# A one-layer encoder block on one core: the experts of the last 32 tokens by gathered rows, and a weight-stationary expert output stage for the other 224

## The chip, the core and the metric

The kernel runs on one core of a Trainium2 chip. The metric is device time in microseconds. The kernel is written in a tile framework: the Python code allocates tiles from pools of buffers and issues operations, and a scheduler gives each engine its fixed order of instructions. Engines: TensorE (PE; its weight loads are listed as PEld), VectorE (DVE), ScalarE (ACT), GpSimd (POOL) and SyncE (SP), which issues the loads of the weights.

## What is computed

One layer on 256 tokens of 2048 features: two token mixers, cross-attention to 256 memory tokens, and a feed-forward layer of 16384 experts of one neuron each, of which every token takes 8 x 16 = 128. The last of these matters here:

```python
def peer_ffn(a, w_pq, sub_keys, expert_u, expert_v):
    ...
    expert = (i1 * PEER_KEYS + i2).astype(jnp.int32)      # T x 8 x 16
    gate = jax.nn.softmax(best_s, axis=-1).astype(t.dtype)
    ...
        u = expert_u[eb]
        pre = jnp.einsum('bd,bed->be', xb, u)
        act = jax.nn.gelu(pre.astype(jnp.float32), approximate=False).astype(xb.dtype) * gb
        return jnp.einsum('be,bed->bd', act, expert_v[eb])
```

`expert_u` and `expert_v` have 16384 rows of 2048 float32 each (134 MB each). The result is added to `h`, and a last RMSNorm follows.

## The kernel before

Every product with weights goes through `wtile` (L82): a tile of 128x2048 float32 (1 MB) is loaded by SyncE's queue into `w` (three buffers), ScalarE casts it to `wh` (L92), and the residual `wl` = `w` - `wh` is formed by VectorE (L94); for the expert input tiles 0 to 63 VectorE takes 1536 columns and GpSimd the other 512 (L97). `wh` and `wl` have two buffers each. The other operand is split in the same way into a high and a low part, and three of the four partial products are summed in PSUM. A number behind `wl` is that of its tile in the order of the code: `wl185` is U's first before and after, and V begins with `wl250` before and `wl252` after.

The experts are computed densely, for all 16384 and all 256 tokens. The input stage U (`u_steps`, L740) runs over 128 tiles of 128 experts. For each of 16 slices of features a pair of matmuls has the weights loaded and the tokens streamed: `wh` against the high and low part of the normed tokens `aT` side by side (512 columns), and `wl` against the high part (256 columns). GELU gives a tile of `P`, 128 experts x 256 tokens; 16 of these make `P0` to `P7`. Beside tiles 0 to 31 the selection of the experts runs on VectorE (`select_steps`), beside tiles 32 to 63 the gates are laid out as a dense matrix (`gate_steps`): one-hot vectors of both halves of an expert's number, eight tokens at a time, f16 matmuls of 128 columns, and stores to the DRAM tensor `gd`. `run_spread` hands out the side work evenly.

The output stage V (`v_steps`, L825) runs over 16 groups `c` of 1024 experts and four slices of 512 features, two weight tiles for each. `gate(c)` (L810) loads the gates of a group and multiplies `P` by them, and the product is split into `ah` and `al`. Here the tokens are the loaded operand and the weights are streamed: 24 matmuls of 512 columns a tile, and VectorE adds the result to `h` after every second tile. The order is U tiles 0 to 63, V quarter 0 (32 tiles), U 64 to 95, V quarter 1, U 96 to 127, V quarters 2 and 3, and the final norm.

Of the kernel before, what the change touches and what calls it, by code (L numbers as in the profile page):

```python
# [9 lines left out]
F32 = mybir.dt.float32  # L10
# [17 lines left out]
TB = 8  # L28


@with_exitstack
def block_kernel(ctx: ExitStack, tc: tile.TileContext, a: dict, out: bass.AP):
# [4 lines left out]
    big = ctx.enter_context(tc.tile_pool(name="big", bufs=6))  # L37
    mid = ctx.enter_context(tc.tile_pool(name="mid", bufs=6))
# [22 lines left out]
    h = const.tile([P, 2, D], F32, tag="h", name="h")  # L61
# [109 lines left out]
    def transpose_split(src, k0, nk, dst, name, gi=None):  # L171

        for kp in range(nk // 2):
# [11 lines left out]
            for kk in range(2):  # L185
                g = gcols[:, gi, k + kk : k + kk + 1]
                ps = pt[:, kk * S : (kk + 1) * S]
                last = nc.scalar.activation(dst[0][:, k + kk, :], ps, AF.Copy, scale=g).ins
                nc.vector.scalar_tensor_tensor(
                    dst[1][:, k + kk, :], ps, g, dst[0][:, k + kk, :].bitcast(F32), op0=ALU.mult, op1=ALU.subtract  # L190
                )
        return last if gi is not None else None

    class Both:


        def __init__(self, name):
            self.tiles = [X([P, NK // 2, 2, S], F32R, f"{name}{i}") for i in range(2)]
# [17 lines left out]
    def norm_steps(name, src, r, gi, dst):  # L216

        xn = X([P, 2, D], F32, f"xn_{name}")
        for q in range(4):
# [3 lines left out]
            transpose_split(xn[:, :, f], 4 * q, 4, dst, name, gi)  # L223
# [225 lines left out]
    def residual(name, w, xT_, ssq_, sides):  # L449

        for f in range(4):
            fs = slice(f * 512, (f + 1) * 512)

            def done(b, ps):
                nc.vector.tensor_tensor(h[:, b, fs], h[:, b, fs], ps, op=ALU.add)
                sumsq(h, b, f, ssq_)

# [152 lines left out]
    residual("mo", a["mem_w_o"], oT, ssq, sides)  # L610
# [8 lines left out]
    gT = const.tile([P, 2, S], F16, tag="gT", name="gT")  # L619
# [30 lines left out]
    aT = Both("a")  # L650
    side = raw_steps("hf", 3, gT_, 3)
    norm = norm_steps("ffn", h, rf_, 3, aT)
# [20 lines left out]
    def select_steps(b):  # L673
# [37 lines left out]
        for s in range(2):  # L711
            for hq in range(4):
# [11 lines left out]
                yield  # L724
        pt = pst(f"pt_sel{b}")
# [3 lines left out]
        t = slice(b * P, (b + 1) * P)  # L729
        nc.vector.tensor_copy(i1T[:, t], pt[:, 0:P])  # L730
        nc.vector.tensor_copy(i2T[:, t], pt[:, P : 2 * P])

        nc.vector.tensor_scalar(gT[:, 0, t], pt[:, 2 * P : 3 * P], GSCALE, None, op0=ALU.mult)
        nc.vector.scalar_tensor_tensor(
            gT[:, 1, t], pt[:, 2 * P : 3 * P], GSCALE, gT[:, 0, t], op0=ALU.mult, op1=ALU.subtract
        )
        yield

# [3 lines left out]
    def u_steps(q):  # L742

        for j in range(32 * q, 32 * q + 32):
            if j % 16 == 0:
                ptiles[j // 16] = X([P, 16, S], F32, f"P{j // 16}")
# [8 lines left out]
            nc.scalar.copy(pre, po[:, S : 2 * S])  # L755
            nc.vector.tensor_tensor(pre, po[:, 0:S], pre, op=ALU.add)  # L756
            nc.scalar.activation(pre, pre, AF.Gelu)  # L757
            yield


    gd = dram.tile([P, 16, 16, 8, 16], F32, tag="gd", name="gd")

    def gate_steps():


        def onehots(t0):
# [5 lines left out]
            o1 = small.tile(sh, F16, tag="o1", name=f"o1_{t0}", bufs=2)  # L772
            eq = small.tile(sh, F16, tag="eq", name=f"eq_{t0}", bufs=1)
# [10 lines left out]
        for t0 in range(0, S, TB):  # L784
# [3 lines left out]
            for q in range(2):  # L788
                ps = psm(f"ps_g{t0}_{q}")
                for n in range(4):  # L790
                    t = 4 * q + n
                    for i in range(2):
                        nc.tensor.matmul(  # L793
                            ps[:, n * P : (n + 1) * P], o1[:, t // 2, :, t % 2], o2[:, i, t // 2, :, t % 2], start=(i == 0), stop=(i == 1)
# [12 lines left out]
            if t0 + TB < S:  # L807
# [3 lines left out]
    def gate(c):  # L811

        n_w[0] += 1
        g = stream.tile([P, 16, 8, 16], F32, tag="w", name=f"w{n_w[0]}", bufs=3)
        nc.sync.dma_start(g, gd[:, c])
        for e in range(2):
            for j in range(4):
                pv = ptiles[c // 2][:, c % 2 * 8 + 4 * e + j, :].rearrange("p (b t) -> p b t", b=16)
                nc.vector.tensor_tensor(pv, pv, g[:, :, 4 * e + j, :], op=ALU.mult)

    ssq_f = new_ssq("final")
    gf = None

    def v_steps(q):

        nonlocal gf
        for c in range(4 * q, 4 * q + 4):
            if c == 15:
                gf = X([P, D], F32, "gf")
                bcast_rows(gf, a["g_final"])  # L830
            ah, al = [], []
            for e in range(2):
                j = 8 * c + 4 * e
                src = ptiles[j // 16][:, j % 16 : j % 16 + 4, :]
                ah.append(M([P, 4, S], F32R, f"ah{c}_{e}"))
                al.append(M([P, 4, S], F32R, f"al{c}_{e}"))
                split(ah[e], al[e], src)
            for ds in range(4):
                po = [acc(f"v{c}_{ds}_{b}") for b in range(2)]
                for e in range(2):  # L840
                    wh, wl = wtile(a["peer_vP"][(c * 4 + ds) * 2 + e], 0)
                    wh = wh.rearrange("p (j f) -> p j f", j=4)
                    wl = wl.rearrange("p (j f) -> p j f", j=4)
                    for j in range(4):
                        for b in range(2):
                            t = slice(b * P, (b + 1) * P)
# [97 lines left out]
```

## Time and profile before

| | us |
|---|---|
| median of 3 runs | 2573.64 |
| lowest, highest | 2573.09, 2575.64 |
| the profiled execution | 2572.24 |
| its span in the trace | 2570.5 |
| TensorE busy | 2540.2 |
| VectorE, ScalarE, GpSimd busy | 1568.8, 1166.1, 176.8 |

The span is cut by its stages: the selection beside U tiles 0 to 31 starts at 1096 us, the gate matrix beside U tiles 32 to 63 fills 1297 to 1481, the first V quarter 1500 to 1674, the third quarter of U 1674 to 1855, and the last V tile ends at about 2558 us. In the rows further down, "PE" is the matmul stream and "PEld" the weight loads, which overlap it. Matmuls are pipelined, so the distance between the starts of two neighbours tells the pace, not the length of one. "idle before" of an engine is time between two of its instructions, with the instruction that released it.

### The profile page before, as it was taken

How to read it: one execution, taken by the hardware profiler on the slowest of the kernel's cores; microseconds unless marked ns; L12 is line 12 of the kernel's file. 1: busy time of each engine (PE TensorE's matmuls, PEld its weight loads, DVE VectorE, ACT ScalarE, POOL GpSimd, SP SyncE). 2: the span in 40 equal slices, each digit the busy share in tenths (PEclk: the TensorE clock that was granted, in tenths of full speed). 3: DMA queues.
4: the chain of work that ended last, by engine and by line, in shares of the span. 5: the costliest groups of instructions: out<-in, count | busy, mean ns of one | idle time of the engine just before them, and what ended most of it. 6: DMA issues, size and time to landing. Idle time of an engine off the chain costs nothing. (4 is left out here: it accounts for less than half of the span.)

```text
span 2570.5 us, 32130 instructions
## 1 busy us (share of the span) xinstructions
PE 2540.2 (99%) x13266; PEld 2158.1 (84%) x13266; DVE 1568.8 (61%) x1877; ACT 1166.1 (45%) x1310; POOL 176.8 (7%) x124
## 2 busy tenths in 40 slices
PE   8999999999999999999999999999999999999998
PEld 7888888888888888888888888888888888888886
DVE  5556544456555455899679866544566544666665
ACT  5454434545444345454455544344443344434443
POOL 0000000000000000022444410000000000000000
PEclk9999999999999999999999999999999999999999
DMA  6554555554544545445567765555565555655663
GB/s 248 186 201 169 182 193 194 215 193 168 191 170 166 177 174 179 168 170 180 181 223 243 245 239 213 207 186 183 211 223 207 193 184 193 233 210 212 229 225 135
DMA packets 74050, 507.66 MB, mean 197 GB/s; under 512 B 8336, under 2 KB 8336, under 8 KB 15152
## 3 DMA queue, kind: packets, MB, share of 16 engines
q1 hardware_dynamic: 67904, 482.37, 52.5%
q0 software_dynamic: 5856, 23.20, 2.9%
q8 instruction: 104, 1.70, 0.3%
q14 instruction: 42, 0.34, 0.0%
q10 hardware_dynamic: 144, 0.03, 0.0%
HBM read 486.70 MB, written 18.87 MB: 197 GB/s over the span
## 5 line engine op out<-in xcount | busy, mean ns | idle before, releaser
L94 DVE TENSOR_TENSOR wl<-w,wh 128x2048 fp32r<-128x2048 f32 (+2 forms) x400 | 863.5, 2164 | 787.2 <-ACT wh L92 787.0
L92 ACT CAST wh<-w 128x2048 fp32r<-128x2048 f32 (+2 forms) x464 | 842.8, 1821 | 911.0 <-PE v L849 362.5
L752 PE MATMUL u<-a,wh 128*128 128x512 f32 x2048 | 725.2, 399 | 0.0
L753 PE MATMUL u<-a,wl 128*128 128x256 f32 x2048 | 574.5, 281 | 5.5 <-DVE wl L97 5.5
L752 PEld LDWEIGHTS u<-a,wh 128*128 128x128 f32 x2048 | 384.6, 188 | 91.5
L850 PE MATMUL v<-wl,ah 128*128 128x512 f32 x1024 | 398.5, 389 | 0.0
L848 PE MATMUL v<-wh,ah 128*128 128x512 f32 x1024 | 398.4, 389 | 0.0
L849 PE MATMUL v<-wh,al 128*128 128x512 f32 x1024 | 398.4, 389 | 0.0
L753 PEld LDWEIGHTS u<-a,wl 128*128 128x128 f32 x2048 | 386.4, 189 | 8.0 <-DVE wl L97 7.9
L850 PEld LDWEIGHTS v<-wl,ah 128*128 128x128 f32 x1024 | 192.2, 188 | 40.3 <-DVE wl L94 0.3
L849 PEld LDWEIGHTS v<-wh,al 128*128 128x128 f32 x1024 | 192.2, 188 | 39.9
L848 PEld LDWEIGHTS v<-wh,ah 128*128 128x128 f32 x1024 | 192.2, 188 | 39.9
L757 ACT ACTIVATE P<-P 128x256 f32<-128x256 f32 x128 | 53.5, 418 | 271.4 <-DVE P L756 271.4
L97 POOL TENSOR_TENSOR wl<-w,wh 128x512 fp32r<-128x512 f32 x64 | 134.8, 2105 | 318.1 <-ACT wh L92 307.1
L97 DVE TENSOR_TENSOR wl<-w,wh 128x1536 fp32r<-128x1536 f32 x64 | 112.6, 1760 | 50.2 <-ACT wh L92 50.2
L854 DVE TENSOR_TENSOR h<-h,v 128x512 f32<-128x512 f32 x128 | 85.2, 684 | 32.6 <-PE v L850 32.6
L116 PE MATMUL g<-wh,x 128*128 128x512 f32 x256 | 100.2, 391 | 0.0
L118 PE MATMUL g<-wl,x 128*128 128x512 f32 x256 | 99.6, 389 | 0.0
L117 PE MATMUL g<-wh,x 128*128 128x512 f32 x256 | 99.6, 389 | 0.0
L138 PE MATMUL qk<-x,wh 128*128 128x512 f32 x256 | 91.0, 400 | 0.2 <-DVE qk L144 0.2
L138 PE MATMUL pq<-hf,wh 128*128 128x512 f32 x256 | 91.0, 399 | 0.0
L138 PE MATMUL mq<-hq,wh 128*128 128x512 f32 x256 | 90.6, 398 | 0.0
(283 smaller groups left out, 3342.8 us busy)
## 6 DMA issues: line engine op xcount, KB each, us to landing
w<-in_peer_uT SPq DMA_DIRECT2D x128, 1024.0 KB, 4.8
w<-in_peer_vP SPq DMA_DIRECT2D x128, 1024.0 KB, 4.8
w<-in_w_in SPq DMA_DIRECT2D x72, 1024.0 KB, 4.8
w<-in_mem_w_kv SPq DMA_DIRECT2D x32, 1024.0 KB, 4.7
w<-in_w_out SPq DMA_DIRECT2D x16, 1024.0 KB, 4.7
w<-in_mem_w_q SPq DMA_DIRECT2D x16, 1024.0 KB, 4.7
w<-in_mem_w_o SPq DMA_DIRECT2D x16, 1024.0 KB, 4.8
w<-in_peer_w_q SPq DMA_DIRECT2D x16, 1024.0 KB, 4.7
```

The lines of the kernel that those rows point to most:

```text
L92: nc.scalar.copy(wh[:, c], w[:, c])
L94: nc.vector.tensor_tensor(wl[:, c], w[:, c], wh[:, c].bitcast(F32), op=ALU.subtract)
L97: e.tensor_tensor(wl[:, c], w[:, c], wh[:, c].bitcast(F32), op=ALU.subtract)
L116: nc.tensor.matmul(po[b], xh, wh[:, k, :], start=(kk == 0), stop=False)
L117: nc.tensor.matmul(po[b], xl, wh[:, k, :], start=False, stop=False)
L118: nc.tensor.matmul(po[b], xh, wl[:, k, :], start=False, stop=(kk == nkc * 4 - 1))
L138: nc.tensor.matmul(po[f], wh[:, k, fs], xT.both(kk), start=(kk == 0), stop=False)
L752: nc.tensor.matmul(po, wh[:, k, :], aT.both(k), start=(k == 0), stop=False)
L753: nc.tensor.matmul(po[:, 0:S], wl[:, k, :], aT[0][:, k, :], start=False, stop=(k == NK - 1))
L848: nc.tensor.matmul(po[b], ah[e][:, j, t], wh[:, j, :], start=first, stop=False)
L849: nc.tensor.matmul(po[b], al[e][:, j, t], wh[:, j, :], start=False, stop=False)
L850: nc.tensor.matmul(po[b], ah[e][:, j, t], wl[:, j, :], start=False, stop=last)
```

## The change

Tokens are divided: `SP` = 32 of them, the last, and `T` = 224.

The 224 stay dense. The matmuls of U have 448 and 224 columns, and `gate_steps` makes 28 groups of one-hot vectors and not 32. `v_steps` now loads the expert weights and streams the tokens: four PSUM tiles of 128 features x 224 tokens, 48 matmuls of 224 columns a weight tile, added by VectorE to `yT` (features x tokens) after every fourth tile. Behind the last tile `yT` is transposed and added to `hx`. `h` is stored to DRAM (`hd`) and reloaded as `hx` late in V; its buffers, and those of `P0` and `P1` (stored to `pd` and reloaded for V's last quarter), go to other tiles. V takes the groups in the order 2, 3, 4, 5, 6, 7, 0, 1 of `P`. `prep_steps` multiplies by the gates and splits for a whole `P` tile (16 tiles of experts) ahead of its use.

The 32 tokens are taken by rows. Partition 32g + t holds token t and a quarter g of its 128 experts, so that 32 steps cover them. Each step gathers 128 rows of `peer_u` by an indirect DMA from GpSimd's queue (1 MB), and VectorE multiplies them by the normed tokens with a sum along the row; after GELU and gate 32 more steps gather rows of `peer_v` and add them, scaled, to one accumulator, which a matmul with `fold` sums over the four quarters into `hx`. Three buffers hold gathered rows (`rows0`'s second half and both halves of `rows1`). `select_steps(1)` now runs ahead of `select_steps(0)` and writes the list of rows and gates `sx`. `run_spread` hands out the 65 steps over the first 168 tiles from V's first on.

```diff
-    big = ctx.enter_context(tc.tile_pool(name="big", bufs=6))
-    mid = ctx.enter_context(tc.tile_pool(name="mid", bufs=6))
+    big = ctx.enter_context(tc.tile_pool(name="big", bufs=7))
+    mid = ctx.enter_context(tc.tile_pool(name="mid", bufs=8))
...
+    def rows_of(src, k):
+        g = bufs[k % 3]
+        nc.gpsimd.indirect_dma_start(
+            g, None, src, bass.IndirectOffsetOnAxis(sx[:, 0, k : k + 1].bitcast(U32), 0)
+        )
+        return g
+
+    def sparse_input():
+        two = [X([P, 2, D], F32, f"rows{i}") for i in range(2)]
+        bufs.extend((two[0][:, 1], two[1][:, 0], two[1][:, 1]))
+        xs = two[0][:, 0]
...
+        nc.vector.scalar_tensor_tensor(xs, xs, rs, gb, op0=ALU.mult, op1=ALU.mult)
+        return xs
+
+    def sparse_steps(xs):
+        for k in range(SP):
+            g = rows_of(a["peer_u"], k)
+            nc.vector.tensor_tensor_reduce(
+                g, g, xs, 1.0, 0.0, op0=ALU.mult, op1=ALU.add, accum_out=act[:, k : k + 1]
+            )
...
+        y = xs
+        for k in range(SP):
+            g = rows_of(a["peer_v"], k)
+            ak = act[:, k : k + 1]
+            if k == 0:
+                nc.vector.tensor_scalar(y, g, ak, None, op0=ALU.mult)
+            else:
+                nc.vector.scalar_tensor_tensor(y, g, ak, y, op0=ALU.mult, op1=ALU.add)
+            yield
...
             for k in range(NK):
-                nc.tensor.matmul(po, wh[:, k, :], aT.both(k), start=(k == 0), stop=False)
-                nc.tensor.matmul(po[:, 0:S], wl[:, k, :], aT[0][:, k, :], start=False, stop=(k == NK - 1))
+                nc.tensor.matmul(po[:, 0 : 2 * T], wh[:, k, :], aT.both(k), start=(k == 0), stop=False)
+                nc.tensor.matmul(po[:, 0:T], wl[:, k, :], aT.tiles[k // 8][:, k % 8, 0], start=False, stop=(k == NK - 1))
...
+    def prep_steps(c):
...
+                nc.vector.tensor_tensor(pv, pv, g[:, :, j, :], op=ALU.mult)
+            yield
+        for e in range(4):
...
+            split(ah, al, pv)
+            parts[c, e] = (ah, al)
+            yield
...
-                    for j in range(4):
-                        for b in range(2):
-                            t = slice(b * P, (b + 1) * P)
-                            first, last = e == 0 and j == 0, e == 1 and j == 3
-                            nc.tensor.matmul(po[b], ah[e][:, j, t], wh[:, j, :], start=first, stop=False)
-                            nc.tensor.matmul(po[b], al[e][:, j, t], wh[:, j, :], start=False, stop=False)
-                            nc.tensor.matmul(po[b], ah[e][:, j, t], wl[:, j, :], start=False, stop=last)
...
+                    for f in range(4):
+                        fs = slice(f * P, (f + 1) * P)
+                        o = po[f][:, 0:T]
+                        for j in range(4):
+                            first, last = e == 0 and j == 0, e == 3 and j == 3
+                            nc.tensor.matmul(o, wh[:, j, fs], ah[:, j, :], start=first, stop=False)
+                            nc.tensor.matmul(o, wh[:, j, fs], al[:, j, :], start=False, stop=False)
+                            nc.tensor.matmul(o, wl[:, j, fs], ah[:, j, :], start=False, stop=last)
...
+    run_spread(u_steps(0), 31, chain(side, select_steps(1), select_steps(0)), 4 + 18 + 18)
+    xs = sparse_input()
+    run_spread(u_steps(1), 27, gate_steps(), T // TB + 1)
+    run(prep_steps(2))
+    rest = chain(
+        v_steps(0),
...
+    run_spread(rest, 168, sparse_steps(xs), 2 * SP + 1)
```

What the scheduler makes of it is another order than the code's. On VectorE, in the first V quarter (`P0` is gated and split beside it), the order before has one residual of a weight tile after another, with single additions to `h` between them:

```order
L94 TENSOR_TENSOR wl250_12032<-w250_12029,wh250_12031 128x2048
L102 TENSOR_TENSOR al0_1_12024<-P0_8005,ah0_1_12023 128x1024
L94 TENSOR_TENSOR wl251_12062<-w251_12059,wh251_12061 128x2048
L756 TENSOR_TENSOR P3_10862<-u63_11966,P3_10862 128x256
L94 TENSOR_TENSOR wl252_12096<-w252_12093,wh252_12095 128x2048
L854 TENSOR_TENSOR h_81<-h_81,v0_0_0_12027 128x512
L854 TENSOR_TENSOR h_81<-h_81,v0_0_1_12028 128x512
L94 TENSOR_TENSOR wl253_12126<-w253_12123,wh253_12125 128x2048
```

The same place after. `ISA` at L789 is the product with a row sum, with a second entry for its column of `act`; L802 and L804 are the scaled sums; a row with x2 stands for two instructions:

```order
L789 ISA rows1_9662,act_8013<-rows1_9662,rows0_9661 128x2048
L789 ISA act_8013 128x1
L789 ISA rows1_9662,act_8013<-rows1_9662,rows0_9661 128x2048
L789 ISA act_8013 128x1
L802 TENSOR_SCALAR rows0_9661<-rows0_9661,act_8013 128x2048
L795 TENSOR_TENSOR act_8013<-act_8013,sx_8012 128x8
L97 TENSOR_TENSOR wl263_12465<-w263_12462,wh263_12464 128x2048
L804 SCALAR_TENSOR_TENSOR rows0_9661<-rows1_9662,act_8013,rows0_9661 128x2048 x2
L804 SCALAR_TENSOR_TENSOR rows0_9661<-rows0_9661,act_8013 128x2048
L804 SCALAR_TENSOR_TENSOR rows0_9661<-rows1_9662,act_8013,rows0_9661 128x2048 x2
L804 SCALAR_TENSOR_TENSOR rows0_9661<-rows0_9661,act_8013 128x2048
L97 TENSOR_TENSOR wl264_12519<-w264_12516,wh264_12518 128x2048
```

The products on `rows1` stand in a row from the residual `wl256` on, the sums follow, and the last sum stands ahead of `wl269`; from there on residuals follow each other as before.

On GpSimd, at the start of `gate_steps`, the order before has its quarters of `wl` and the stores of the gate matrix:

```order
L97 TENSOR_TENSOR wl217_9644<-w217_9641,wh217_9643 128x512
L97 TENSOR_TENSOR wl218_9694<-w218_9691,wh218_9693 128x512
L97 TENSOR_TENSOR wl219_9768<-w219_9765,wh219_9767 128x512
L97 TENSOR_TENSOR wl220_9842<-w220_9839,wh220_9841 128x512
L97 TENSOR_TENSOR wl221_9916<-w221_9913,wh221_9915 128x512
L804 DMA gd_8003<-gs0_0_9733 128x8x128
L804 DMA gd_8003<-gs0_1_9734 128x8x128
```

And after:

```order
L100 TENSOR_TENSOR wl215_9566<-w215_9563,wh215_9565 128x512
L766 DMA rows0_9661<-in_peer_u,sx_8012 128x2048
L100 TENSOR_TENSOR wl216_9621<-w216_9618,wh216_9620 128x512
L766 DMA rows0_9661<-in_peer_u,sx_8012 128x2048 x2
L100 TENSOR_TENSOR wl218_9680<-w218_9677,wh218_9679 128x512
L766 DMA rows0_9661<-in_peer_u,sx_8012 128x2048
L100 TENSOR_TENSOR wl219_9729<-w219_9726,wh219_9728 128x512
L841 DMA pd_8014<-P1_8852 128x3584
L766 DMA rows0_9661<-in_peer_u,sx_8012 128x2048
L100 TENSOR_TENSOR wl220_9802<-w220_9799,wh220_9801 128x512
L766 DMA rows0_9661<-in_peer_u,sx_8012 128x2048
```

Gathers into the one free buffer in `rows0` moved between these quarters of `wl`; eleven products of them stand on VectorE between `wl214` and `wl225`. Those into `rows1` wait until its buffer of the pool is free.

## Rows read from the trace of the kernel before

**Rows 1.** The page's totals: busy us, share and instructions of each engine.

```profile
span 2570.5 us, 32130 instructions
...
PE 2540.2 (99%) x13266; PEld 2158.1 (84%) x13266; DVE 1568.8 (61%) x1877; ACT 1166.1 (45%) x1310; POOL 176.8 (7%) x124
```

**Rows 2.** Waits of TensorE: line, releaser: us in all, times, longest.

```profile
PE pt_x L178 <- DMA h<-in_x: 8.5, 2, 5.2
PE u L753 <- DVE wl L97: 5.5, 7, 1.1
```

**Rows 3.** Windows: us, busy of PE, PEld, DVE, ACT, POOL, clock, DMA share, GB/s.

```profile
1096.30:1230.00 133.70, 129.07 (x735) 111.36 (x734) 129.96 (x344) 65.92 (x77) 36.15 (x23) 1.00 0.48 171
1230.00:1297.00 67.00, 66.12 (x377) 57.17 (x377) 33.82 (x38) 28.84 (x34) 30.99 (x12) 1.00 0.52 188
...
1500.00:1674.20 174.20, 174.20 (x770) 144.03 (x769) 110.29 (x96) 67.65 (x40) 0.00 (x0) 1.00 0.59 213
1674.20:1855.10 180.90, 180.90 (x1025) 156.81 (x1025) 89.59 (x75) 84.15 (x96) 0.00 (x0) 1.00 0.54 192
2558.00:2570.50 12.50, 0.56 (x3) 0.13 (x1) 4.22 (x9) 3.39 (x7) 0.72 (x1) 0.61 0.49 168
```

**Rows 4.** Timeline of TensorE, V: start, duration, engine, line, operation, output and inputs.

```profile
1502.21 0.39 PE L848 MATMUL v<-wh,ah 128*128 128x512 f32 x1
...
1511.28 0.39 PE L849 MATMUL v<-wh,al 128*128 128x512 f32 x1
```

**Rows 5.** Timeline of TensorE, matmuls of 256 columns in cross-attention.

```profile
732.77 0.28 PE L521 MATMUL ps_ms<-kTh,mq 128*128 128x256 f32 x1
...
735.51 0.28 PE L523 MATMUL ps_ms<-kTh,mq 128*128 128x256 f32 x1
```

**Rows 6.** Timeline of TensorE: weight loads in a row, and the gate matrix's matmuls.

```profile
1025.19 0.53 PEld L637 LDWEIGHTS ps_s<-skT,pqT 128*128 128x128 f32 x4
...
617.90 0.91 PEld L178 LDWEIGHTS pt_hq<-ident,h 128*128 128x128 f32 x8
...
1304.01 1.11 PE L793 MATMUL ps_g<-o,o 128*128 128x128 f16 x16
```

**Rows 7.** Timeline of ScalarE and VectorE, one weight tile of V.

```profile
1500.11 1.91 ACT L92 CAST wh<-w 128x2048 fp32r<-128x2048 f32 x1 [0.75 <-PE u L752]
...
1502.05 2.29 DVE L94 TENSOR_TENSOR wl<-w,wh 128x2048 fp32r<-128x2048 f32 x1 [0.48 <-ACT wh L92]
```

**Rows 8.** VectorE by line and shape: busy us, mean ns; idle before, releaser.

```profile
L94 DVE TENSOR_TENSOR wl<-w,wh 128x2048 fp32r<-128x2048 f32 x360 | 825.1, 2292 | 760.7 <-ACT wh L92 760.7
L97 DVE TENSOR_TENSOR wl<-w,wh 128x1536 fp32r<-128x1536 f32 x64 | 112.6, 1760 | 50.2 <-ACT wh L92 50.2
L778 DVE TENSOR_TENSOR o<-eq,gT 128x1024 f16<-128x1024 f16 x64 | 51.9, 851 | 0.5
L776 DVE TENSOR_TENSOR o<-iotax,i1T 128x1024 f16<-128x1024 f16 x32 | 37.4, 1170 | 18.8 <-PE ps_g L793 18.8
...
L776 DVE TENSOR_TENSOR eq<-iotax,i2T 128x1024 f16<-128x1024 f16 x32 | 22.1, 690 | 0.9
L723 DVE TENSOR_REDUCE sel<-oh 128x32 f32<-128x512 f32 x16 | 10.7, 673 | 0.0
```

**Rows 9.** DMA issues (the last: 1390 to 1500 us): KB each, us to landing.

```profile
w<-in_peer_vP SPq DMA_DIRECT2D x128, 1024.0 KB, 4.8
...
mem<-in_mem POOLq DMA_DIRECT2D x2, 1024.0 KB, 8.5
...
w<-in_peer_uT SPq DMA_DIRECT2D x13, 1024.0 KB, 6.6
```

**Rows 10.** Windows of the highest rate found; GB/s is the last column.

```profile
1304.00:1304.92 0.92, 0.92 (x18) 0.92 (x17) 0.89 (x2) 0.79 (x1) 0.00 (x0) 1.00 0.85 312
732.77:735.51 2.74, 2.74 (x25) 2.74 (x24) 0.68 (x1) 1.91 (x1) 0.00 (x0) 1.00 0.88 308
```

**Rows 11.** One line of GpSimd: min, median, max ns of an issue.

```profile
L467 POOL DMA_DIRECT2D mem<-in_mem x2: 536/557/578, 486.8 to 487.4; - x2
```

More of the change, by code (lines that the diff above doesn't have):

```diff
@@ L194, in block_kernel, with __init__ @@
     class Both:
-        def __init__(self, name):
-            self.tiles = [X([P, NK // 2, 2, S], F32R, f"{name}{i}") for i in range(2)]
+        def __init__(self, name, n=S):
+            self.tiles = [X([P, NK // 2, 2, n], F32R, f"{name}{i}") for i in range(2)]
         def both(self, k):
@@ L456, in done @@
                 sumsq(h, b, f, ssq_)
+                if keep is not None:
+                    nc.gpsimd.dma_start(keep[b * P : (b + 1) * P, fs], h[:, b, fs])
             run(dense(f"{name}{f}", w, f, xT_, 4, done), sides(f))
@@ new lines, in block_kernel @@
+    hx = None
+    bufs = []
+    def rows_of(src, k):
[8 more added lines that the diff above has]
+        xs = two[0][:, 0]
+        rs = small.tile([P, 1], F32, tag="rs", name="rs", bufs=1)
+        n_w[0] += 1
+        gb = stream.tile([P, D], F32, tag="w", name=f"w{n_w[0]}", bufs=3)
+        bcast_rows(gb, a["g_ffn"])
+        for g in range(NG):
+            p = slice(g * SP, (g + 1) * SP)
+            nc.gpsimd.dma_start(xs[p], hd[T:S])
+            nc.gpsimd.dma_start(rs[p], rf_[P - SP : P, 1:2])
+        nc.vector.scalar_tensor_tensor(xs, xs, rs, gb, op0=ALU.mult, op1=ALU.mult)
+        return xs
@@ L783, in gate_steps @@
         gs = None
-        for t0 in range(0, S, TB):
+        for t0 in range(0, T, TB):
             if t0 % 16 == 0:
@@ L806, in gate_steps @@
                     )
-            if t0 + TB < S:
+            if t0 + TB < T:
                 made = onehots(t0 + TB)
             yield
[L811 to L816, printed above, removed]
-            for j in range(4):
-                pv = ptiles[c // 2][:, c % 2 * 8 + 4 * e + j, :].rearrange("p (b t) -> p b t", b=16)
-                nc.vector.tensor_tensor(pv, pv, g[:, :, 4 * e + j, :], op=ALU.mult)
+    parts = {}
@@ new lines, in prep_steps @@
+    def prep_steps(c):
+        if c not in ptiles:
+            ptiles[c] = X([P, 16, T], F32, f"P{c}b")
+            nc.gpsimd.dma_start(ptiles[c], pd[c])
+        pt = ptiles[c]
+        for b in range(2):
+            n_w[0] += 1
+            g = stream.tile([P, T // 16, 8, 16], F32, tag="w", name=f"w{n_w[0]}", bufs=3)
+            nc.sync.dma_start(g, gd[:, 2 * c + b])
+            for j in range(8):
+                pv = pt[:, 8 * b + j, :].rearrange("p (b t) -> p b t", t=16)
+                nc.vector.tensor_tensor(pv, pv, g[:, :, j, :], op=ALU.mult)
+            yield
+        for e in range(4):
+            ah = M([P, 4, T], F32R, f"ah{c}_{e}")
+            pv = pt[:, 4 * e : 4 * e + 4, :]
+            al = M([P, 4, T], F32R, f"al{c}_{e}")
+            split(ah, al, pv)
+            parts[c, e] = (ah, al)
+            yield
@@ L821, in block_kernel @@
     ssq_f = new_ssq("final")
+    yT = None
     gf = None
+    order = [2, 3, 4, 5, 6, 7, 0, 1]
     def v_steps(q):
-        nonlocal gf
-        for c in range(4 * q, 4 * q + 4):
-            if c == 15:
+        nonlocal gf, hx, yT
+        for n in range(2 * q, 2 * q + 2):
+            c = order[n]
+            if n == 0:
+                yT = X([P, NK, T], F32, "yT")
+            if n == 6:
+                hx = X([P, 2, D], F32, "hx")
+                for b in range(2):
+                    nc.gpsimd.dma_start(hx[:, b, :], hd[b * P : (b + 1) * P, :])
+            if n == 7:
```

152 lines of the change are left out of this document (101 added, 51 removed).

## The prediction

> **What bounds the kernel now.** I read the page's busy totals first, then who TensorE waited for, then the stages, and only there the starts of single matmuls. TensorE is busy 2540.2 of 2570.5 us [rows 1], and its largest waits are 8.5 us for the first input and 5.5 us for a residual tile [rows 2]; nothing else feeds the span. In the part that the change touches, the expert input stage U (tiles 0 to 31 beside the selection, 32 to 63 beside the gate matrix, 64 to 127 alone) and the expert output stage V, the stages are full too [rows 3]: 32 output tiles in 174.2 us (5.44 us a tile) and 32 input tiles in 180.9 us (5.65 us; 512 pairs of a 512 and a 256 column matmul, 353 ns a pair). So time goes down only where TensorE gets less to stream, and goes up wherever TensorE must wait.
>
> What TensorE waits for next is the weight tile. A tile is loaded, cast by ScalarE to `wh`, and the residual `wl` is then formed by VectorE: 1.91 us and 2.29 us, one behind the other [rows 7]. `wh` and `wl` have two buffers each, so the cast of a tile cannot start before TensorE has left the tile two before it. 4.2 us of a tile's 5.44 are thus taken, and VectorE may be about 1 us late before TensorE stops. VectorE executes in the order of its program. That is the point to look at.
>
> **The change part by part.**
>
> *TensorE, input stage.* The two matmuls of a pair shrink from 512 and 256 columns to 448 and 224. 40 matmuls of 512 columns start 226.8 ns apart (9.07 us over 40) [rows 4]; 23 of 256 columns start 119.1 ns apart [rows 5]; that is 0.421 ns a column and 11.4 ns beside it. 96 columns fewer are 40 ns, 353 becomes 313. No row has 224 columns with a new weight load each. Below 256 columns the load may bound: four loads of the same 128x128 f32 shape follow each other in 0.53 us, the last taking 0.19, so 113 ns apart; eight with the transposes in 0.91 us, about 110 apart [rows 6]. Ends for a 224 column matmul: 106 ns by the columns, 119 as the 256 column row. I take 110, the weight loads' own pace, as nearest. A pair is then 317 ns and a tile 16 x 36 = 0.58 us shorter (0.43 to 0.64). Tiles 64 to 127 gain 37 us. Tiles 32 to 63 gain 19, and 4 from 64 fewer f16 matmuls (1.11 us for 16, so at most 69 ns each [rows 6]). Among tiles 0 to 31 VectorE is busy 129.96 of the first 133.7 us [rows 3] and its selection work is unchanged, so only the last 67 us, some 12 tiles, gain: 7. Together 67 us (51 to 73).
>
> *TensorE, output stage.* 24 matmuls of 512 columns become 48 of 224, now with the expert weights loaded and the tokens streamed. 48 x 110 ns is 5.28 us against 5.44: 128 tiles gain 21 us; at 106 ns 48, at 119 ns the stage loses 35. So the rewritten stage streams 12.5% fewer products but issues twice the loads, and gives back nearly all of it.
>
> *The 32 sparse tokens.* 64 gathers of 128 rows of 8 KB (1 MB each), 32 products with a row sum, one scaling, 31 scaled sums, all over 128x2048 f32. No such gather and no such product is in the trace. The plain residual of the same shape takes 2292 ns [rows 8]: one end, 2.3. The other is a second pass for the sum, 4 x 673 ns by the 512 column reduction [rows 8], so 5.0. I take 2.3, since the built order has one instruction of that shape for each product, with one of a single column behind it. 65 of these, with the scaling of the inputs, are some 150 us of VectorE, whose idle time would hold them if they came one per two or three tiles, as `run_spread` hands them out. The built order does not spread them. The fences on the change show it: after tile 256 VectorE has 21 products, the scaling and 31 sums in one block, with five or six between two `wl`, and the block ends only at `wl269`. Each product waits for its gather, and each gather for the buffer that an earlier product frees. Behind each of them on VectorE waits the next `wl`, and behind that TensorE.
>
> The price of that block goes by turns of a buffer. A 1 MB load lands 4.8 us after its issue for the weight tiles, 6.6 in the gate stage, 8.5 for the two `mem` loads on GpSimd's queue [rows 9]; GpSimd's issue takes 0.56 us [rows 11]. Taking 6.6, a buffer's turn is 0.6 + 6.6 + 2.3 = 9.5 us. The 21 products use two buffers: 4.75 us each, 100 us (4.8 and 2.3: 81; 8.5 and 5.0: 148). The 31 sums use three: 3.2 us by turns, but six sums and a weight tile are 7 MB, and the highest rate in a stretch that I found is 312 GB/s [rows 10], 3.36 us a MB, so 3.9 us each: 121 us (2.7 where only VectorE binds: 84; 121 at the top). TensorE has 11 tiles to do meanwhile, 58 us. Loss 100 + 121 - 58 = 163 us (107 to 211).
>
> The Trainium skill (DMA: Bandwidth & Descriptors, Anatomy of one DMA — SWDGE (gpsimd) path) puts such a transfer at about 2.0 us plus its bytes over 436 GB/s, an estimate of 4.4 us for 1 MB; the `mem` row has 8.5, so rule and row differ. By the rule a product is 3.4 us and a sum 2.8, the block would lose 99 us and the gate stage 28, and the sum below would be about 2620.
>
> *The same in the gate stage.* Eleven products share one buffer, between `wl214` and `wl225` (the POOL fence: gathers between GpSimd's quarters of `wl`, so GpSimd's share waits behind them too). The first gather is early; ten turns of 9.5 us and 5 us for scaling the inputs are 100 us, against 50 us for TensorE's nine tiles with their gate matmuls. Loss 50 us (4.8 us landing: 32; 8.5 and 5.0: 96).
>
> *The rest.* Gate multiplications and splits before the first output tile now come as a whole quarter, 16 x 0.4 us and four splits, partly behind input tiles; transposes and adds behind the last tile; the clock. TensorE falls to a granted 0.61 in the last 12.5 us, where it is busy for 0.56 [rows 3], and full speed elsewhere; in the block it would work about a quarter of the time. At the lower level of 1.2 GHz a tile takes twice 5.3 us, which still fits between two late `wl`. 9 us for all (0 to 15). Saving `h` to memory, the two stored `P` tiles and the fold lie on idle queues: nothing, and 1 us each if not.
>
> Sum on the profiled execution (2572.24; the median of the runs is 2573.64, 0.05% away): 2572 - 67 - 21 + 163 + 50 + 9 = 2706, say 2707. All low ends give about 2590, all high ends about 2880.
>
> **The rivals.**
> *A. The gathers always come in time,* and the block costs only VectorE's own work: 52 x 2.3 + 11 x 2.3 + 3 for gate multiplications = 148, minus 58, so 90 us; in the gate stage VectorE has 65 us of work (11 products and the scaling, nine `wl` of 1.76, nine adds of 0.4, five sets of one-hots of 3.6 [rows 8]) against TensorE's 50, so 15 us. 2572 - 88 + 90 + 15 + 9 = 2598. For it: POOL issues ahead as buffers free up. Against: 8.5 us landing, and 7 MB for six sums.
> *B. Gathers or products dearer,* at the high ends: 2572 - 88 + 211 + 96 + 9 = 2800. For it: building 128 addresses from a list is in no row.
> *C. Weight loads at 119 ns:* 224 columns cost what 256 cost. 51 - 35 = 16 us gain in place of 88: 2778. For it: loads and starts both stand at 119 in the 256 column rows; against: 110 and 113 in rows of the same load.
> *D. Faster.* The second of two matmuls on one loaded `wh` starts without a gap, so that only columns count, 94 ns. A `v` tile is 4.5 us (gain 119), a pair 353 - 40 - 23 = 290, input tiles gain 1.0 us (about 115): 2572 - 234 + 222 = 2560. It decides from about 97 ns on, where gain and loss of 222 us meet. Against it: every matmul in the trace has its own weight load, also where two neighbours share the operand, and 11.4 ns come with 512 columns as with 256. The Trainium skill (TensorE: Matmul & The Clock Gate, Back-to-back issue gap) has columns over 2.4 and 2.5 ns, so 96 ns for 224 and 216 for 512; the trace has 226.8 for 512, which speaks for the longer gap here.
>
> **How the numbers follow.** Forecast 0.52 (2650 to 2760), B 0.18, C 0.13, A 0.12, D 0.05. The range 2595 to 2830 takes in A and C and half of B, and leaves D and B's tail, under 0.2. A measurement of this kernel can tell about 0.2% (5 us) from no change. Faster 0.05 (D), same 0.02 (between D and A), slower 0.93.
>
> **What would show it.** In the profile after: TensorE's idle time put down to `wl` on VectorE, about 160 us in the first output quarter and about 50 early in the gate stage; slices there with TensorE busy for a quarter; products and sums near 2.3 us that wait for DMA; all later V tiles near 5.3 us and U tiles near 5.07. Wrong if TensorE stays full in the first output quarter (the block is covered), if the gathers land in under 4 us (A), or if matmuls of 224 columns start far from 110 ns apart (C, D).

## The result, and the profile after

The changed kernel takes 2867.17 us (median of 4 runs, 2864.39 to 2871.77) against 2573.36: 1.114 times the time before, 95% interval 1.112 to 1.116. The direction was forecast, the size was not: 294 us were lost where 134 were forecast, and the time lies above the range.

The page of the changed kernel, busy totals:

```profile
span 2862.6 us, 38540 instructions
...
PE 2546.0 (89%) x16314; PEld 2330.4 (81%) x16314; DVE 1648.3 (58%) x1961; ACT 1154.2 (40%) x1314; POOL 305.7 (11%) x216
```

Against [rows 1] TensorE's idle time went from 30.3 us (2570.5 less 2540.2) to 316.6: 286 of the 292 us that the span grew. Its busy time is the same within 6 us, though it has an eighth fewer columns to stream in U and V; where that gain went is told under "Wrong third". Whom TensorE waited for (us in total, times, longest), changed kernel:

```profile
PE v L958 <- DVE wl L97: 145.6, 18, 20.2
PE u L835 <- DVE wl L100: 60.9, 17, 8.3
PE ps_g L877 <- DVE o L862: 46.2, 26, 13.6
PE v L956 <- ACT yT L962: 14.1, 2, 8.0
```

In [rows 2] the residuals cost 5.5 us, here over 200. A stage begins with its first expert matmul, and these are the distances of the starts, in us; e1, e6 and e11 are kernels of the next section:

| stage | before | after | e1, no sparse part | e6, order by hand, no sparse part | e11, order by hand, complete |
|---|---|---|---|---|---|
| U 0 to 63 | 403.7 | 502.0 | 435.2 | 395.6 | 405.4 |
| first V quarter | 174.3 | 344.0 | 182.2 | 176.4 | 177.0 |
| U 64 to 95 | 180.9 | 170.6 | 172.4 | 166.8 | 171.6 |
| second V quarter | 174.1 | 180.7 | 183.1 | 172.6 | 173.3 |
| U 96 to 127 | 180.9 | 170.5 | 170.0 | 165.2 | 167.6 |
| last two V quarters | 348.4 | 387.3 | 373.5 | 348.0 | 360.9 |

The same by windows of the changed kernel (columns as in [rows 3]: us, busy of PE, PEld, DVE, ACT, POOL, granted clock, DMA share, GB/s), the first of them inside the selection:

```profile
1110.00:1210.00 100.00, 66.26 (x339) 59.98 (x339) 96.07 (x258) 32.15 (x39) 18.13 (x14) 0.85 0.30 107
...
1296.00:1420.00 124.00, 73.44 (x432) 67.35 (x431) 74.19 (x77) 32.20 (x55) 38.92 (x29) 0.78 0.65 231
...
1616.00:1720.60 104.60, 45.10 (x274) 43.47 (x274) 61.95 (x59) 9.92 (x14) 31.38 (x20) 0.67 0.72 268
1731.50:1841.90 110.40, 33.03 (x198) 32.11 (x197) 82.22 (x37) 12.45 (x11) 52.44 (x28) 0.63 0.81 312
...
1845.00:1940.41 95.41, 95.41 (x849) 95.41 (x849) 48.16 (x36) 35.22 (x23) 0.00 (x0) 0.99 0.55 193
...
2462.19:2849.51 387.32, 364.83 (x3108) 360.15 (x3107) 203.22 (x203) 135.00 (x90) 0.53 (x1) 0.96 0.52 188
```

The third and fourth are the block that was forecast: TensorE is busy for 45 of 104.6 us beside the products and 33 of 110.4 beside the sums, and full right behind them. The first was not forecast: VectorE is busy for 96 of 100 us with selection and residuals, and TensorE for 66. In the last, 22 us are lost in waits and more at a lower clock.

The sparse instructions, by line of the changed kernel (min/median/max ns, first and last start; then what VectorE waited for ahead of them: us, times):

```profile
L789 DVE CUSTOM_DVE_ANT_0 rows<-rows,rows x21: 2280/2293/2293, 1618.4 to 1718.3; 128x2048 f32<-128x2048 f32 x21
L789 DVE CUSTOM_DVE_ANT_0 rows<-rows x11: 2284/2292/2293, 1300.7 to 1402.5; 128x2048 f32<-128x2048 f32 x11
...
  DMA rows<-in_peer_u,sx: 86.1, 23
...
L804 DVE SCALAR_TENSOR_TENSOR rows<-rows,act,rows x21: 2345/2352/2353, 1731.6 to 1841.7; 128x2048 f32<-128x2048 f32 x21
...
  DMA rows<-in_peer_v,sx: 34.2, 16
...
L766 POOL DMA_INDIRECT rows<-in_peer_u,sx x32: 937/1102/3065, 1240.6 to 1711.6; - x32
L766 POOL DMA_INDIRECT rows<-in_peer_v,sx x32: 935/2082/3647, 1405.1 to 1833.5; - x32
```

And how long a gather takes to land (median us from issue, the last column):

```profile
rows<-in_peer_u,sx POOLq DMA_INDIRECT x32, 7.2
rows<-in_peer_v,sx POOLq DMA_INDIRECT x32, 7.7
```

A product takes 2.29 us, as the plain residual in [rows 8] does; a gather lands in 7.2 to 7.7 (medians), between the 6.6 and 8.5 of [rows 9], and GpSimd needs a median of 1.10 us to issue one from `peer_u` and 2.08 from `peer_v`, two to four times [rows 11]. The Trainium skill's figures (DMA: Bandwidth & Descriptors, Anatomy of one DMA — SWDGE (gpsimd) path), from which the prediction worked out an estimate of 4.4 us for 1 MB, don't fit these gathers.

The pace of the new output stage, two of its matmuls 40 starts apart in an undisturbed stretch, and of the input stage, two starts 16 pairs (one tile) apart (timeline of TensorE, changed kernel, as [rows 4]):

```profile
1899.88 0.28 PE L956 MATMUL v<-ah,wh 128*128 128x224 f32 x1
...
1904.34 0.28 PE L957 MATMUL v<-al,wh 128*128 128x224 f32 x1
...
1989.92 0.38 PE L834 MATMUL u<-a,wh 128*128 128x448 f32 x1
...
1994.93 0.38 PE L834 MATMUL u<-a,wh 128*128 128x448 f32 x1
```

4.46 us over 40 are 111.5 ns a matmul and 5.35 us a tile of V, against 5.44 before. A tile of U takes 5.01 us, against 5.65.

### The profile page after: what moved, and what is told of

It reads as the page before. It is cut to its first block, busy times and chain, and to the rows that moved or that the text cites. A ratio compares the mean times of both kernels' runs of the same rounds, so it can differ in the third digit from the quotient of the medians.

```text
span 2862.6 us, 38540 instructions
## 1 busy us (share of the span) xinstructions
PE 2546.0 (89%) x16314; PEld 2330.4 (81%) x16314; DVE 1648.3 (58%) x1961; ACT 1154.2 (40%) x1314; POOL 305.7 (11%) x216
## 5 line engine op out<-in xcount | busy, mean ns | idle before, releaser
L958 PE MATMUL v<-ah,wl 128*128 128x224 f32 x2048 | 582.8, 285 | 145.6 <-DVE wl L97 145.6
L834 PE MATMUL u<-a,wh 128*128 128x448 f32 x2048 | 679.8, 388 | 3.4 <-ACT wh L95 3.4
L835 PE MATMUL u<-a,wl 128*128 128x224 f32 x2048 | 558.8, 273 | 74.2 <-DVE wl L100 60.9
L956 PE MATMUL v<-ah,wh 128*128 128x224 f32 x2048 | 582.3, 284 | 24.0 <-ACT yT L962 14.1
L957 PE MATMUL v<-al,wh 128*128 128x224 f32 x2048 | 577.9, 282 | 0.0
L958 PEld LDWEIGHTS v<-ah,wl 128*128 128x128 f32 x2048 | 411.7, 201 | 149.1 <-DVE wl L97 149.1
L956 PEld LDWEIGHTS v<-ah,wh 128*128 128x128 f32 x2048 | 411.9, 201 | 26.5 <-ACT yT L962 14.5
L957 PEld LDWEIGHTS v<-al,wh 128*128 128x128 f32 x2048 | 411.3, 201 | 0.5 <-issue 0.5
L839 ACT ACTIVATE P<-P 128x224 f32<-128x224 f32 x128 | 50.1, 391 | 371.0 <-DVE P L838 371.0
L141 PE MATMUL mk<-mem,wh 128*128 128x512 f32 x256 | 89.7, 396 | 0.0
```

Of the source, the lines that this page charges most:

```text
L141: nc.tensor.matmul(po[f], wh[:, k, fs], xT.both(kk), start=(kk == 0), stop=False)
L834: nc.tensor.matmul(po[:, 0 : 2 * T], wh[:, k, :], aT.both(k), start=(k == 0), stop=False)
L835: nc.tensor.matmul(po[:, 0:T], wl[:, k, :], aT.tiles[k // 8][:, k % 8, 0], start=False, stop=(k == NK - 1))
L956: nc.tensor.matmul(o, wh[:, j, fs], ah[:, j, :], start=first, stop=False)
L957: nc.tensor.matmul(o, wh[:, j, fs], al[:, j, :], start=False, stop=False)
L958: nc.tensor.matmul(o, wl[:, j, fs], ah[:, j, :], start=False, stop=last)
```

## The experiments

Three theories were held against each other: the loss is a matter of VectorE's order; it comes from the gathers themselves (traffic, landing); it comes from the output stage. Each kernel was run beside the kernel before on the same chip (2572.6 to 2573.7 us). Numbers without an interval are single runs; the kernels that were run four to ten times spread over 6 to 8 us.

**e1: no sparse part.** The calls of `sparse_input` and `sparse_steps` are taken out.

```diff
-    xs = sparse_input()
...
-    run_spread(rest, 168, sparse_steps(xs), 2 * SP + 1)
+    run(rest)
```

> The changed kernel without its sparse part: the last 32 tokens get no expert output (no gathers, no products, no fold). The rest of the code is untouched. Theory: the loss has three sources that are all a matter of VectorE's order, the block of sparse operations, the selection that stands closer together among the first 13 tiles of U, and gate multiplications that stand ahead of two residuals and wait for their load; each wait is made longer by TensorE's lower clock behind it. Without the sparse block and its part in the gate stage (about 176 and 75 us by the stages of the profile after) the time should be 2616 us (2595 to 2640), so still slower than before by about 40, with the waits of the selection (some 35 us) and behind the gate multiplications still there. Rival (the rows): all of the loss comes from the gathers and their products; then 2574 - 80 - 13 = 2480 us.

2629.05 us. So the sparse part costs 238 us, and without it the kernel is still 56 us slower than before, inside the range of the theory of the order. In the table the sparse part is 162 us of the first V quarter (344.0 less 182.2) and 67 of U's first half.

**e2: the sparse steps pinned.** A step's VectorE instructions get an order edge behind the last residual handed out before it, so the scheduler can't draw them forward.

```diff
+                last_wl[0] = nc.vector.tensor_tensor(wl[:, c], w[:, c], wh[:, c].bitcast(F32), op=ALU.subtract).ins
...
-                next(side, None)
+                with tc.issue_after(last_wl[0]):
+                    next(side, None)
```

> The whole computation; each sparse step's VectorE instructions must now stand behind the residual of the tile beside which the code hands them out, one every two or three tiles from the first V quarter on. Theory (the order costs, not the work): 64 products and sums of 2.3 us fit into the 3.07 us that VectorE idles between two residuals in V, so the time is that of the kernel without a sparse part, 2616 us, within 25. Rival (the gathers cost bandwidth or VectorE time wherever they stand): 2700 us or more.

2675.86 us: the same work, the same gathers, 191 us less. The order is most of the price of the sparse part, but not all: 47 us over e1 are left where 25 were allowed for, so the time lies above the expected one.

**e3: no gathers.**

```diff
-        nc.gpsimd.indirect_dma_start(
-            g, None, src, bass.IndirectOffsetOnAxis(sx[:, 0, k : k + 1].bitcast(U32), 0)
-        )
         return g
```

> The changed kernel with its 64 gathers left out; the products and sums run over buffers that are set to zero once, so the experts of the last 32 tokens are not computed. The built order then puts all 63 products and sums into the gate stage, tiles 214 to 239, where VectorE was busy for 158 of 184 us before. Theory: 63 x 2.3 = 147 us more of VectorE there, less some 25 us that it has free, so a loss of about 120 on top of 2616: 2735 us (2700 to 2770); what separates this from 2867 is the waiting for gathers. Rival (waiting for gathers is all): 2616 us.

2755.96 us, in the expected range. With nothing to wait for, the scheduler draws all products and sums into U's first half, which takes 555.5 us, 120 more than in e1; the first two V quarters are as in e1, the last two take 12 us more. So VectorE's own 147 us, out of place, cost 120 here without any gather. The changed kernel's remaining 111 us go with the gathers, but its order is another one too, so this is no clean split.

**e4: all of it pinned.** As e2 for selection, gate matrix and sparse steps; and the multiplication by the gates is moved one tile behind the issue of its load, behind that tile's residual. The steps that this adds are handed out beside two more tiles.

```diff
             nc.sync.dma_start(g, gd[:, 2 * c + b])
-            for j in range(8):
-                pv = pt[:, 8 * b + j, :].rearrange("p (b t) -> p b t", t=16)
-                nc.vector.tensor_tensor(pv, pv, g[:, :, j, :], op=ALU.mult)
+            yield
+            with tc.issue_after(last_wl[0]):
+                for j in range(8):
+                    pv = pt[:, 8 * b + j, :].rearrange("p (b t) -> p b t", t=16)
+                    nc.vector.tensor_tensor(pv, pv, g[:, :, j, :], op=ALU.mult)
             yield
```

> The whole computation with an order set by hand: sparse steps, selection steps and gate steps stand behind the residual of the tile that hands them out, and the multiplication by the gates stands one tile behind the issue of its load, behind that tile's residual. Theory: TensorE stays busy everywhere, so 2574 - 80 (U tiles 0.63 us shorter) - 13 (V tiles 0.1 us shorter) + 8 for the first gate multiplications of V + 10 at the end = about 2500 us (2480 to 2530), faster than before by 3%. Rival (gathers or the new output stage cost by themselves): over 2600 us.

2581.58 us, 1.004 times before (1.002 to 1.005). 286 us came back by order alone, but not the 367 that would have made it 2500. TensorE's largest waits in e4:

```profile
PE ps_g L879 <- DVE o L864: 20.2, 26, 3.2
PE u L837 <- DVE wl L101: 15.6, 8, 5.0
PE v L960 <- DVE yT L968: 14.4, 8, 2.4
```

The third is new: the next slice of features waits for additions to `yT` that free its four PSUM accumulators, and these stand behind a product or a sum.

**e5: the price of one wait.** The kernel before, with a residual formed several times at eight places in V.

```diff
-                nc.vector.tensor_tensor(wl[:, c], w[:, c], wh[:, c].bitcast(F32), op=ALU.subtract)
+                for _ in range(1 + late):
+                    nc.vector.tensor_tensor(wl[:, c], w[:, c], wh[:, c].bitcast(F32), op=ALU.subtract)
```

> The kernel before, with one residual in each of the last eight groups of V formed 2, 3, 3, 4, 4, 5, 7 and 9 times in place of once (the same values; 2.29 us each), so that VectorE is late by a known amount at eight places. With the 3.1 us that VectorE idles between residuals TensorE's waits should be about 0, 1.5, 1.5, 3.8, 3.8, 6.1, 10.7 and 15.2 us, 43 together. Theory (a wait costs more than itself, because TensorE runs at the lower granted clock behind it): 2574 + 43 + 6 or 7 places of 2.5 us = about 2634 us. Rival (a wait costs itself): 2617 us.

2661.97 us. The waits were longer than estimated from VectorE's idle time:

```profile
PE v L853 <- DVE wl L95: 68.6, 7, 20.6
```

The last two V quarters took 434.8 us, 86.4 more than before: the seven waits, and 17.8 us besides, 2.5 each on average, as the theory had it; the total lies above the expected one because the waits were longer. What the 17.8 us are shows behind the first of the seven, a wait of 3.48 us that ended at 2272.55 (windows of e5, columns as above):

```profile
2255.00:2269.00 14.00, 14.00 (x63) 11.30 (x61) 9.82 (x6) 4.86 (x3) 0.00 (x0) 1.00 0.41 151
2269.00:2272.50 3.50, 0.07 (x1) 0.00 (x0) 3.50 (x5) 0.88 (x1) 0.00 (x0) 0.79 0.00 0
...
2272.55:2274.50 1.95, 1.95 (x5) 1.58 (x6) 1.95 (x1) 0.00 (x0) 0.00 (x0) 0.50 0.53 134
2274.50:2276.50 2.00, 2.00 (x6) 1.59 (x5) 0.20 (x1) 0.00 (x0) 0.00 (x0) 0.50 1.06 426
2276.50:2278.50 2.00, 2.00 (x7) 1.58 (x6) 1.28 (x4) 0.00 (x0) 0.00 (x0) 0.66 0.98 401
2278.50:2280.50 2.00, 2.00 (x10) 1.62 (x10) 1.50 (x5) 0.78 (x1) 0.00 (x0) 1.00 0.22 90
```

TensorE counts as busy throughout, but starts 5 and 6 matmuls in 2 us at a granted 0.50 (the level of 1.2 GHz), and 10 at 1.00. Behind the seven waits the clock stays at 0.50 for 3.3 to 6.2 us, 33 us together; at half the pace that is 16 of the 17.8 us.

**e6 and e7: the dense part alone, order by hand, at 224 and at 256 tokens.** e4 without the calls of e1; e7 has `T = S` besides.

> The kernel of e4 (order set by hand) without its sparse part: the last 32 tokens get no expert output. It tells what the sparse part costs at its best so far. Theory (sums in V delay the additions to yT, and with them the four accumulators that the next slice of features waits for): the V quarters come down to 5.35 us a tile, so 2582 - 37 = about 2544 us (2530 to 2555). Rival (spread operations are free, the loss in e4 is the output stage's own): 2580 us.

> As e6, but with all 256 tokens dense (512 and 256 columns in U, 48 matmuls of 256 columns a tile in V): the weight-stationary output stage alone, at the old number of tokens; the whole computation. Theory (columns decide, 119 ns for 256): U as before, V 5.71 us a tile, so slower than e6 by some 60 + 48: about 2652 us (2630 to 2680), slower than before by 3%. Rival (weight loads decide, 110 ns for both): U 60 us longer than e6 and V the same, 2605 us.

2535.69 and 2627.56 us. e6 is the best that the dense part gives here, in the expected range: 38 us less than before, where the prediction's terms made 88. The sparse part still costs e4 46 us more, a little over the theory. e7 ends just below its range. It has the new output stage at the old number of tokens, and loses 54 us, 46 of them in V: in it matmuls of 256 columns start 120 ns apart (timeline of e7, again 40 starts):

```profile
1559.94 0.28 PE L960 MATMUL v<-ah,wh 128*128 128x256 f32 x1
...
1564.74 0.28 PE L961 MATMUL v<-al,wh 128*128 128x256 f32 x1
```

5.76 us a tile against 5.44, as expected. e7 is 92 us over e6 where 108 were expected: 32 tokens less shorten U's first half by only 16 us, and its second half by 30. Columns still count below 256, but weakly: 120 to 111.5 ns for 32 columns fewer.

**e8: e2 without its gathers** (the edit of e3).

> The kernel of e2 (sparse steps pinned, the rest as the scheduler orders it) without its gathers: products and sums run over zeroed buffers. e2 is 47 us above e1, which has no sparse part. Theory (VectorE's place in the queue costs, not the 64 MB): about 2670 us. Rival (the gathers' traffic and landing cost): 2630 to 2640 us.

2660.86 us, nearer to the theory than to the rival. Of the 47 us between e1 and e2, 32 are VectorE's operations where they stand and 15 go with the gathers; with single runs the 15 is rough.

**e9: e4 with eight accumulators and chosen places.** Every second slice takes PSUM buffers of the transposes; sparse steps go to tiles of V and U without other VectorE work; the first gate multiplications start beside U's last four tiles.

```diff
+                if ds % 2:
+                    po = [(pst if f < 2 else psm)(f"v{c}_{ds}_{f}") for f in range(4)]
+                else:
+                    po = [acc(f"v{c}_{ds}_{f}") for f in range(4)]
...
+                    if n in (1, 3):
+                        yield e in (0, 2)
+                    elif n < 7:
+                        yield (ds, e) in ((0, 0), (0, 2), (1, 2), (2, 2))
```

> e4 with three more changes, the whole computation: in V every second slice of features takes its four accumulators from the PSUM buffers that transposes and small matmuls use elsewhere, so that eight are in turn; sparse steps go only to tiles of V and U that carry no gate multiplication, no splits and no additions to yT (64 such tiles); the gate multiplications for the first V quarter start beside the last four tiles of U before it. Theory (in e4 the sums delay the additions to yT and the multiplications, each with a stretch at the lower clock behind it): most of the 46 us between e4 and e6 comes back, 2548 us (2538 to 2562), faster than before by 1%. Rival (a sum beside a residual costs wherever it stands, by VectorE's or the gathers' traffic): 2575 us or more.

2572.42 us, 0.9998 of before (0.9989 to 1.0008): 9 us less than e4, but 10 us above the expected range. The waits for `yT` are gone, the last two V quarters take 362.4 us and not 369.7; but U's first half got 11 us longer. There a gate multiplication stood ahead of a residual again and waited for its load (waits of VectorE, e9):

```profile
DVE P L917 <- DMA w<-gd: 6.7, 1, 6.7
```

**e10: e9 with one set of one-hot vectors per tile.** The residual of a tile of U 32 to 63 is held behind the vectors of the tile before.

```diff
+                with tc.issue_after(hold[0]) if hold[0] is not None and e is nc.vector else nullcontext():
+                    i = e.tensor_tensor(wl[:, c], w[:, c], wh[:, c].bitcast(F32), op=ALU.subtract).ins
```

> e9 with one more order: beside tiles 32 to 63 of U the residual of a tile stands behind the one-hot vectors of the tile before, so that VectorE makes one set of them per tile and not two sets every second tile. Theory (TensorE's 20 us of waits for one-hot vectors in e6 come from that pairing, and the stage gains nothing from fewer columns because of it): 10 to 15 us less than e9. Rival (the stage is bound by VectorE's or ScalarE's sum of work): the same as e9 within 4 us.

2631.6 us, 1.023 times before (1.021 to 1.024): 59 us worse than e9, which neither theory nor rival had. The waits for one-hot vectors did not go, they doubled (waits of TensorE, e10):

```profile
PE ps_g L881 <- DVE o L866: 39.1, 28, 2.8
```

The edit also holds residuals back, so it does not show whether the pairing caused the waits in e6. What bounds this stage is left open.

**e11: e9 with the first gate multiplications back behind U.**

> e9 with the gate multiplications of the first V quarter back behind the last tile of U (as in e4), the whole computation. In e9 they stood ahead of the residual of U's last tiles and waited 6.7 us for their load; U's tiles 56 to 64 lost 14 us there, in e4 6 us. Theory: about 8 us less than e9, 2564 us (2560 to 2568), so just faster than before. Rival (the 14 us come from the gate matrix's end and stay): 2572 us.

2567.38 us, 0.9976 of before (0.9966 to 0.9986). That is in the expected range, the fastest complete kernel of the study, 0.2% under the kernel before and 300 us under the change as made.

## Why the prediction was wrong

The forecast was a sum of three parts, and the runs measure each: the dense part's gain, forecast 88 us, is 38 in e6; the sparse part's loss, forecast 163 + 50 = 213, is 238 (changed kernel less e1); and 93 us (e1 less e6) were lost by selection, gate steps and gate multiplications in the built order, for which the forecast had only its 9 us for "the rest". 50 + 25 + 93 - 9 make 159 of the 160 us between 2707 and 2867. The step that failed is thus the one that took the order of the older side work as unchanged and put its waits at nothing beyond those 9 us; the dense gain and the sparse loss were mis-sized besides.

**Right: the block, and its turns.** 21 products took 102 us (100 forecast), 31 sums 112 (121), TensorE did 10.7 tiles meanwhile (512 matmuls of 48 a tile; 11), and the sparse part lost 162 us in that quarter (163). The reason given for the sums, a highest rate of 312 GB/s, did not hold: that was the mean beside them, and shorter windows below show 414 to 429. So the nearness of this term is in part luck. In the gate stage the products took 104 us (100). Rival A fell, since products waited 86 us for gathers; B did, by 7.2 us and 2.29 us; C and D did, by 111.5 ns: nearer to the 110 taken than to 119 or 94. (Two workings in the rivals and the rule are slightly off without bearing on this: by its own terms D breaks even at about 95 ns and not 97, and the 3.4 us of a product by the rule leave out the issue.)

**Wrong first: "its selection work is unchanged, so only the last 67 us, some 12 tiles, gain: 7".** The work was unchanged, its order was not. The built order puts it between the first 13 residuals of U (`wl185` to `wl197`), where the kernel before has it between 24; VectorE is full over 100 us in place of 134 [rows 3], with about twice as much selection ahead of each residual. Counted from U's start, e4, where the selection is spread, passes tile 28 33 us earlier than e1. The prediction read the order at two places and took the rest to be as in the code. Why the scheduler packed it stays open: with the two calls of `select_steps` exchanged back the built order is as dense, and that the larger `mid` pool lets more selection tiles live at once is a guess that no run tests.

**Wrong second: the gate multiplications, "partly behind input tiles", in 9 us for all the rest.** They are cheap but stand one residual earlier than before. VectorE waited for such a load at 15 places, 71 us in all (waits of VectorE, changed kernel):

```profile
DVE P L913 <- DMA w<-gd: 51.1, 11, 6.5
...
DVE P0b L913 <- DMA w<-gd: 10.7, 2, 6.1
DVE P1b L913 <- DMA w<-gd: 9.1, 2, 4.6
```

One of them (timelines of VectorE and, last, of ScalarE; the bracket is the idle time ahead and its releaser):

```profile
2470.43 2.29 DVE L97 TENSOR_TENSOR wl<-w,wh 128x2048 fp32r<-128x2048 f32 x1 [3.57 <-ACT wh L95]
...
2478.99 2.51 DVE L913 TENSOR_TENSOR P<-P,w 128x224 f32<-128x224 f32 x8 [6.27 <-DMA w<-gd]
2481.42 4.49 DVE L97 TENSOR_TENSOR wl<-w,wh 128x2048 fp32r<-128x2048 f32 x2
...
2473.85 1.91 ACT L95 CAST wh<-w 128x2048 fp32r<-128x2048 f32 x1 [3.45 <-PE v L957]
```

The gates' load goes into the `w` buffer that the residual at 2470.43 frees, is issued at its end, and lands 6.3 us later. The residual behind the multiplication could have run from 2475.76 on, when its cast had ended. The kernel before has one more residual ahead of the same multiplication, which then waits for nothing (timeline of VectorE, kernel before):

```profile
2217.64 2.29 DVE L94 TENSOR_TENSOR wl<-w,wh 128x2048 fp32r<-128x2048 f32 x1 [2.77 <-ACT wh L92]
...
2223.08 2.29 DVE L94 TENSOR_TENSOR wl<-w,wh 128x2048 fp32r<-128x2048 f32 x1 [1.08 <-ACT wh L92]
2225.29 2.77 DVE L819 TENSOR_TENSOR P<-P,w 128x256 f32<-128x256 f32 x8
```

In the changed kernel each of the 12 such waits from 2065 us on is followed by a wait of TensorE of 2.5 to 4.3 us, 39 us together. From e1 to e6 the stages behind U's first half get 52 us shorter, and there only these multiplications, and the splits behind them, were moved.

**Wrong third: the clock, "still fits between two late `wl`".** It does in the block, where VectorE sets the end. Behind a single wait it doesn't. Behind the wait above, in the changed kernel (windows):

```profile
2475.00:2479.40 4.40, 4.40 (x40) 4.27 (x39) 0.41 (x2) 0.99 (x2) 0.00 (x0) 1.00 0.49 201
2479.40:2483.70 4.30, 0.06 (x1) 0.00 (x0) 4.30 (x9) 1.66 (x1) 0.00 (x0) 0.73 0.19 50
2483.76:2485.00 1.24, 1.24 (x6) 1.24 (x7) 1.24 (x1) 0.00 (x0) 0.00 (x0) 0.50 1.01 429
2485.00:2487.00 2.00, 2.00 (x11) 2.00 (x11) 1.29 (x2) 0.00 (x0) 0.00 (x0) 0.50 1.05 414
2487.00:2489.00 2.00, 2.00 (x15) 2.00 (x15) 0.38 (x1) 0.00 (x0) 0.00 (x0) 0.70 1.17 311
2489.00:2491.00 2.00, 2.00 (x21) 2.00 (x20) 0.39 (x2) 0.00 (x0) 0.00 (x0) 1.00 0.79 332
```

A wait of 4.3 us is followed by over 4 us at half the pace. e5 prices that at 2.5 us a wait. It also shows in the totals, since TensorE counts as busy at either level. e4 has the same 16314 matmuls in the same shapes (page of e4):

```profile
PE 2482.2 (96%) x16314; PEld 2272.5 (88%) x16314; DVE 1659.4 (64%) x1961; ACT 1153.9 (45%) x1314; POOL 310.4 (12%) x216
```

That is 64 us less than in the changed kernel, whose mean granted clock is 0.945 against 0.991. So the fewer columns did save TensorE time, and the lower clock took it back. How the 64 us divide is not shown: in the block, where VectorE sets the end, they need not have cost time, and behind single waits e5 shows that they do.

**Terms of the wrong size.** The paces were right: 5.01 us for a tile of U (5.07 forecast) and 5.35 for one of V (near 5.3). But in U's first half the gain of 23 us for tiles 32 to 63 did not come even without a sparse part and with the order set by hand: counted from U's start, e6 is 12 us ahead of the kernel before at tile 32 and 9 at tile 63. TensorE waits for one-hot vectors there, 20 us in e4 and e6. The sparse operations cost 67 us in U's first half and not 50. Of V's 21 us (12 by the measured pace) e6 shows none in all: the first quarter loses 2.1, the others gain 1.5 and 0.4. And the sparse part is not free where it is spread: e11 is 32 us over e6.

By stages the miss is 78 us in U's first half (98 lost where 20 were forecast), 12 in the first V quarter, 28 in U's second half and the second V quarter, 49 in the last two: 167, less the 9 for the rest that was counted apart. The largest part of the miss, the 93 us from e1 to e6, was neither gathers nor products but older steps that the scheduler had moved.

## What to carry to other kernels

When a change alters buffers or side work under a scheduler, compare the built order of the bounding engine's supplier over the whole program, stage by stage and not only where new instructions appear: count what stands between two of the instructions that feed the bound. An instruction that waits for a DMA should stand behind everything that is ready before its data; an order edge to the last feeding instruction brought 286 of 294 us back without touching the work. And price a wait of TensorE at more than its length.

## What the runs showed of the hardware

- After the seven waits of 3.5 to 20.6 us in e5 TensorE's granted clock was 0.50 for 3.3 to 6.2 us, and a wait cost 2.5 us beyond itself on average. In the changed kernel three waits of 2.5 to 2.8 us left no such stretch (the 4 us behind those that ended at 2080.33, 2130.74 and 2431.51 us have a granted 1.00).
- Matmuls with a new weight load each start 111.5 ns apart at 224 columns and 120 at 256, against 226.8 at 512 [rows 4]. The Trainium skill (TensorE: Matmul & The Clock Gate, Back-to-back issue gap) gives a formula for the gap of a single matmul, by which 224 columns would take 96 ns, an estimate; the trace decides.
- The highest rate is above the 312 GB/s of [rows 10]: 414 to 429 GB/s over 1 to 2 us in the windows above. Over the 110 us of the sums the mean was 312.
- A gather of 1 MB landed in 7.2 to 7.7 us (medians) in the changed kernel, and in 5.9 to 9.6 where the steps were spread (e2, e4, e11).
